# Down projection of two token groups as seven products in a stage of its own, its operands kept in device memory

## The chip, the core and the metric

The kernel runs on one NeuronCore of a Trainium2 chip. A core has a matrix engine (PE), which multiplies a stationary weight tile of 128x128 with a moving tile of 128 x n and adds into one of eight PSUM banks, three engines for elementwise work (DVE, ACT and POOL), and SP, which in this kernel only issues DMA transfers, in the order in which they stand on its queue. Each engine works through its own queue in order and waits on semaphores for the others. The metric is the device time of one execution in microseconds. Before the change the runs shown took 1119.27 and 1119.56 us, median 1119.41 us.

## The reference, cut to what matters

One layer of a decoder trunk for 1056 tokens (1024 of a prompt and 8x4 samples), D_MODEL = 1024, D_FF = 2816, all in fp32. The change lies in the last third of it:

```
def _rms(x, g):
    y = xf * lax.rsqrt(jnp.mean(xf * xf, axis=-1, keepdims=True) + EPS)
    return y * g

    ...                                     # mixing sub-layer gives x
    f = _rms(x, n_ffn_pre)
    f = (jax.nn.silu(f @ w_gate) * (f @ w_up)) @ w_down
    x = x + _rms(f, n_ffn_post)
    x = x + jax.nn.sigmoid(x @ w_ple_gate) * (p @ w_ple)
```

`w_gate` and `w_up` are 1024x2816, `w_down` is 2816x1024, `w_ple_gate` is 1024x1024, `w_ple` is 256x1024.

## The kernel before, in words

**Tiles.** Channels lie on the 128 partitions, tokens on the free axis. The 1056 tokens are three groups of 352: groups 0, 1 and 2. An fp32 product is made of three passes of a reduced format: every operand is split into a high part (a CAST on ACT, L164) and a low part (a subtraction on DVE, L165), and `gemm` (L291) issues for each 128x128 weight tile three matmuls of 128x352: high by high, high by low, low by high. In the profile a line "b<-hid,wh" is a matmul into a PSUM bank `b` with the moving tile `hid` (a hidden chunk) and the weight tile `wh`; "wl" is the low part of a weight, "fh" and "fl" the parts of the normalised input.

**Seven products.** Gate and up projection of groups 0 and 1 are made together: the two groups are the two columns, and two halves of 512 channels the two rows, of a 2x2 block product, which is made with seven block products in place of eight. Their operands are block sums made beforehand (`f7`: B11, B21, B22, T1 to T4), and the sums of weights come from POOL (`w_sums`, L1010). The same is done for the last product, x @ w_ple_gate, in the tail (`e7`, `ple_first`, `ple_rest`). Group 2 is always computed directly.

**The walk.** The 22 hidden chunks of 128 are taken in 11 slabs of two. `WALK` (L209) lists which slab is computed for which groups: slabs 0 to 4 for group 2; slabs 5 to 10 for all groups; slabs 0 to 4 for groups 0 and 1. For each item `gate_up` (L1026) makes the hidden chunk and writes it, split, to `hid`. Behind the first gate product of the next item `downs` (L1175) makes the down projection of the item before: for each of the eight output chunks m and each group in it, `down` (L1093) issues 2 chunks x 3 passes = 6 matmuls and adds the bank to the sum `o` (DVE, L1107; the first time a copy on ACT). So the down projection of groups 0 and 1 is 2 x 8 x 22 x 3 = 1056 matmuls, spread over the last eleven items, that of group 2 is 528.

**The tail.** When a group's sums are complete, `ple_steps` (L1136) makes its second normalisation: the squares are added up in `acc` (L813, L814), a ones matrix times `acc` on PE gives the mean (`rstd_steps`, L313), DVE scales (L1152), multiplies by the gain `gn` and adds the residual (L1156). The residual x was written to device memory earlier (`x1d<-x`) and is read back (`x<-x1d`, L1147). Then come the products with `w_ple_gate` and `w_ple`, the sigmoid, and the store of y.

**What sets the order.** PE runs its matmuls in the order written. `chain` puts the steps of a normalisation in line beside it: `turn(n)`, called behind each product, gives them n matmuls of progress, and a step that asks for 24 goes on when 24 matmuls have been issued. `need(k)` (L270) prepares weights ahead: it issues the load on SP (`w_load`, a raw tile `wr`, three slots), and the split of item k + LOOK on ACT and DVE. Raw tiles and `act_tile`s (tag "a", 28 slots of 128x1408) are reused, so a load or a split can wait for the last reader of a slot.

Of the kernel before, what the change touches and what calls it, by code (L numbers as in the profile page):

```python
# [10 lines left out]
F32 = mybir.dt.float32  # L11
F32R = mybir.dt.float32r
# [49 lines left out]
def trunk_kernel(  # L62
# [43 lines left out]
    def nm(s):  # L106
        cnt[0] += 1
        return f"{s}{cnt[0]}"
# [109 lines left out]
    def direct_item(src, shape):  # L218
        return item("direct", add_plan(src, shape))

    WGU, WD = [], []
    for s, gs in WALK:
        pairs_of = []
        for i in range(SLAB):
            c = SLAB * s + i
            jg = direct_item(w_gu[c, 0], [P, KC, P])
            if 0 not in gs:
                ju = direct_item(w_gu[c, 1], [P, KC, P])
            if i == 0 and WD:
# [7 lines left out]
        WD.append(None)  # L237
    WPE = [[], []]
# [5 lines left out]
    FIRST = 1  # L244
    for m in range(FIRST):
        plan_ple(0, m)
    WD[-1] = [direct_item(w_dn[WALK[-1][0], j], [P, SLAB, 512]) for j in range(2)]
    for m in range(FIRST, KC):
        plan_ple(0, m)


# [14 lines left out]
        W2[a] = wp0, item("half", jb), item("sums", ja, jb)  # L266

    made = {}

    def need(k, ahead=LOOK):  # L270

        for i in range(len(made), min(k + ahead + 1, len(ITEMS))):
            kind, js = ITEMS[i]
            if kind in ("direct", "home"):
                w_split(js[0], act_tile if kind == "home" else None)
                made[i] = pairs[js[0]]
            elif kind == "half":
                w_load(js[0])
                t = w_tile([P, KC, P], "w2")
                made[i] = t[:, 0:4, :], t[:, 4:8, :]  # L280
                split(*made[i], raws[js[0]][:, 4:8, :])
            else:
                for j in js:
                    w_load(j)
                made[i] = w_sums(*(raws[j] for j in js))
            for kind, js in ITEMS[i + 1 : i + 3]:
                for j in js:
                    w_load(j)
        return made[k]

    def gemm(ps, ops, start=True, stop=True):  # L291
# [698 lines left out]
    share[0] = 0.45  # L990


    hid = [None] * G

    new_hid = [None] * G

    def hid_put(g, slot, ht):
        split(new_hid[g][:, slot, :], new_hid[g][:, SLAB + slot, :], ht)

    def w_sums(a1, a2):  # L1000

# [21 lines left out]
    def quarter(w, h):  # L1023
        return tuple(t[:, 4 * h : 4 * h + 4, :] for t in w)

    def gate_up(items, slot, gs, pending):  # L1026

        ig, iu, is_ = items
        n = N

        def product(w, x):
            ps = bank()
            gemm(ps[:, :n], ops4(w, x))
            turn(12)
            return ps[:, :n]

        def direct(w):
            ps = bank()
            gemm(ps[:, :n], ops8(w, fs[2]))
            turn(24)  # L1040
            return ps[:, :n]

        def add(out, a, ps):
            ve.tensor_tensor(out, a, ps, op=ALU.add)
# [17 lines left out]
        for g in gs:  # L1062
            if slot == 0:
                new_hid[g] = half(g, F32R, "hid")
        if 2 in gs:
            hid_put(2, slot, sl)
# [8 lines left out]
        u3 = tmp(n, "u3")  # L1075
        add(u3, p1, product(s["S3"], f7["T3"]))
        c21 = tmp(n, "c21")
# [4 lines left out]
        hid_put(0, slot, c21)  # L1082
# [4 lines left out]
        se.activation(p1, p1, AF.Silu)  # L1087
        ve.tensor_tensor(u3, u3, p1, op=ALU.mult)
        hid_put(1, slot, u3)

    os_ = [None] * G

    def down(n, m, g):  # L1093
        wh, wl = need(WD[n][m // 4], 0 if n == len(WALK) - 1 else LOOK)
        cols = slice((m % 4) * P, (m % 4 + 1) * P)
        ps = bank()
        v = ps[:, : NS[g]]
        gemm(v, [(wh[:, k, cols], wl[:, k, cols], hid[g][:, k, :], hid[g][:, SLAB + k, :]) for k in range(SLAB)])
        turn(6)
        if os_[g] is None:  # L1100
            os_[g] = [half(g, s="o") for h in range(2)]
        o = os_[g][m // 4][:, m % 4, :]
        if (g, m) not in begun:
            begun.add((g, m))
            se.copy(o, v)
        else:
            ve.tensor_tensor(o, o, v, op=ALU.add)  # L1107
# [4 lines left out]
    pls = [None] * G  # L1112
    acc3 = [None] * G

    def last_down(n, m, g):
        down(n, m, g)
        if m == 0:
            acc3[g] = acc_tile(g)
        squares_into(acc3[g], os_[g][m // 4][:, m % 4, :], m == 0)


    e7 = {}
# [13 lines left out]
    def ple_steps(g):  # L1136
# [9 lines left out]
            x2[g][h] = half(g, s="x2")  # L1146
            nc.sync.dma_start(x2[g][h], x1d[g][h])  # L1147
        r = yield from rstd_steps(acc3[g], 28)
        behind = tc.keep_in_program_order if g == 2 else lambda ins: ins
        for h in range(2):  # L1150
            yh, xh = os_[g][h], x2[g][h]
            behind(ve.tensor_tensor(yh, yh, bc4(r), op=ALU.mult))  # L1152
            for c in range(4):
                k = 4 * h + c
                behind(
                    ve.scalar_tensor_tensor(  # L1156
                        xh[:, c, :], yh[:, c, :], gn[:, 3, k : k + 1], xh[:, c, :], op0=ALU.mult, op1=ALU.add
                    )
                )
                if g == 2 and c % 2:  # L1160
                    yield 6, 0
            yield 12 if g == 2 else 24, 0
            if g == 2:
                x2s[g].append(f_operand(xh, g))
            elif (g, h) != (1, 0):
                e7[f"B{h + 1}{g + 1}"] = f_operand(xh, g)
            yield 10, 0
# [2 lines left out]
                e_sum(name)  # L1170
                yield 20, 0

    END = len(WALK) - 1

    def downs(n):  # L1175
        s, gs = WALK[n]
        hid[:] = old_hid
        for half_m in (range(4), range(4, KC)):
            for g in (2, 0, 1):
                for m in half_m:  # L1180
                    if g in gs:
                        (last_down if g == 2 and s == NSLAB - 1 else down)(n, m, g)
        if s == NSLAB - 1:
            share[0] = 0.1
            chain(ple_steps(2), 19)

    for n, (s, gs) in enumerate(WALK):
        if n == AHEAD:
            finish(list(chains))
        old_hid = list(new_hid)  # L1190
        for i in range(SLAB):
            gate_up(WGU[n][i], i, gs, (lambda: downs(n - 1)) if i == 0 and n else None)
    finish(list(chains))
    share[0] = 0.7


    early = {}

# [85 lines left out]
            add(p1, p1, product(s["S4"], e7["B22"]))  # L1284
        ple_end(p1, wp, a, 1)

    hid[:] = new_hid
    for m in range(FIRST):
        ple_out(m, 2)
# [6 lines left out]
    for m in range(FIRST):  # L1296
        embed_early(WPE[0][m][0], m, 0)
    for m in range(FIRST, KC):
        ple_out(m, 2)
        embed_early(WPE[0][m][0], m, 0)  # L1300
    finish(chains[:1])
    for a in (7, 5, 3, 1):
        ple_first(a)
    for m in range(4):
# [90 lines left out]
```

## Time and profile before

| | |
|---|---|
| runs shown | 1119.27 and 1119.56 us, median 1119.41 |
| profiled execution | 1118.45 us, span 1116.7 us |
| granted clock of PE | 0.998 of full speed |
| PE busy | 1098.3 us, 98% of the span, 6999 instructions |
| DVE busy | 778.4 us, 70% |
| ACT busy | 458.8 us, 41% |
| POOL busy | 201.2 us, 18% |
| DMA | 101.79 MB, mean 91 GB/s |

A PE matmul line gives a mean of about 322 ns, but matmuls overlap in the pipeline, so the time that one costs is the distance between two starts, not its duration. The busy time of a window counts overlapping matmuls once. "PE b L126 <- DVE acc L814: 0.8, 1, 0.8" in the view of waits reads: matmuls of line 126 waited for the DVE instruction of line 814 that wrote `acc`, 0.8 us in all, once, at the longest 0.8 us.

### The profile page before, as it was taken

The numbers are of one execution on the slowest core, as the hardware profiler recorded it, in microseconds if no ns is written. First come the engines' busy times: TensorE is split into PE (matmuls) and PEld (weight loads), VectorE is DVE, ScalarE is ACT, GpSimd is POOL, SyncE is SP. The second block draws the span as 40 slices with busy tenths as digits, with TensorE's granted clock in tenths as the row PEclk, the third lists the DMA queues.
The fourth block names the chain that finished last, engine by engine and source line by source line (L and its number), as shares of the span: only waits on it lengthen the run. The fifth ranks groups of instructions, "written<-read, shape, count | busy, mean of one in ns | idle before, by whom it ended". The sixth has DMA issues, their size and how long they took to land.

```text
span 1116.7 us, 17519 instructions
## 1 busy us (share of the span) xinstructions
PE 1098.3 (98%) x6999; PEld 1080.0 (97%) x6999; DVE 778.4 (70%) x1296; ACT 458.8 (41%) x823; POOL 201.2 (18%) x169
## 2 busy tenths in 40 slices
PE   9999999999999999999999999999999999999987
PEld 8999988899999999999999999999999999999976
DVE  6766388877979864355565555657867877789887
ACT  8322268655645433331322213133424324366442
POOL 1045022100000221020111102012231132200242
PEclk9999999999999999999999999999999999999999
DMA  8121310542644212021120202114212212246242
GB/s 289 57 70 38 115 56 20 202 157 95 221 147 132 77 57 77 20 76 38 38 77 22 73 20 76 39 38 140 77 38 95 77 57 95 95 156 209 64 129 89
DMA packets 35986, 101.79 MB, mean 91 GB/s; under 512 B 4260, under 2 KB 14916, under 8 KB 35904
## 3 DMA queue, kind: packets, MB, share of 16 engines
q1 hardware_dynamic: 34576, 98.90, 26.3%
q10 hardware_dynamic: 1328, 1.77, 0.5%
q8 instruction: 55, 0.90, 0.3%
q14 instruction: 27, 0.22, 0.1%
HBM read 90.55 MB, written 10.11 MB: 90 GB/s over the span
## 4 chain that ended last, share of the span: by engine, by line
PE 82%; DVE 6%; POOL 3%; ACT 3%; issue 2%; DMA 2%; ACTq 0%; SPq 0%; POOLq 0%; DVEq 0%
PE b L126 81%; POOL wr L1010 3%; DVE wl L165 1%; DVE sl L165 1%; ACT sh L164 1%; DMA xr<-in_x_dram 1%; PE b L120 1%; DVE o L1133 1%; ACT h L394 1%; DVE sg L1223 1%; DVE yo L1225 1%; DMA wr<-in_w_pg_dram 0%; ACT wh L164 0%; DMA wr<-in_w_gu_dram 0%; ACT a L664 0%
## 5 line engine op out<-in xcount | busy, mean ns | idle before, releaser
L126 PE MATMUL b<-hid,wh 128*128 128x352 f32 x1056 | 253.1, 322 | 2.3 <-ACT hid L164 1.6
L164 ACT CAST wh<-wr 128x1024 fp32r<-128x1024 f32 (+1 forms) x135 | 138.8, 1030 | 252.7 <-PE b L126 203.4
L126 PE MATMUL b<-fh,wh 128*128 128x352 f32 x712 | 229.9, 323 | 0.0
L126 PE MATMUL b<-fh,wl 128*128 128x352 f32 x712 | 228.3, 321 | 0.0
L126 PE MATMUL b<-fl,wh 128*128 128x352 f32 x712 | 228.2, 320 | 0.0
L1010 POOL TENSOR_TENSOR wr<-wr 128x512 f32<-128x512 f32 x52 | 75.0, 1442 | 736.1 <-DVE wl L165 453.4
L165 DVE TENSOR_TENSOR wl<-wr,wh 128x1024 fp32r<-128x1024 f32 (+1 forms) x135 | 165.5, 1229 | 43.3 <-ACT wh L164 42.8
L126 PEld LDWEIGHTS b<-hid,wh 128*128 128x128 f32 x1056 | 182.7, 188 | 3.6 <-ACT hid L164 1.9
L126 PE MATMUL b<-hid,wl 128*128 128x352 f32 x528 | 169.3, 321 | 0.0
L126 PE MATMUL b<-fh,sh 128*128 128x352 f32 x416 | 134.7, 324 | 3.5 <-ACT sh L164 1.3
L126 PE MATMUL b<-fh,sl 128*128 128x352 f32 x416 | 133.7, 321 | 2.2 <-DVE sl L165 2.2
L1107 DVE TENSOR_TENSOR o<-o,b 128x352 f32<-128x352 f32 x240 | 115.3, 517 | 29.1 <-PE b L126 28.9
L126 PEld LDWEIGHTS b<-fl,wh 128*128 128x128 f32 x712 | 134.0, 188 | 0.0
L126 PEld LDWEIGHTS b<-fh,wh 128*128 128x128 f32 x712 | 133.5, 187 | 0.0
L126 PEld LDWEIGHTS b<-fh,wl 128*128 128x128 f32 x712 | 133.4, 187 | 0.0
L126 PE MATMUL b<-fl,sh 128*128 128x352 f32 x416 | 133.4, 321 | 0.0
L165 DVE TENSOR_TENSOR sl<-wr,sh 128x1024 fp32r<-128x1024 f32 x52 | 63.6, 1223 | 82.3 <-ACT sh L164 82.1
L164 ACT CAST sh<-wr 128x1024 fp32r<-128x1024 f32 x52 | 53.9, 1046 | 146.3 <-POOL wr L1010 103.2
L126 PE MATMUL b<-h,wh 128*128 128x352 f32 x480 | 105.5, 326 | 0.8 <-ACT h L394 0.8
L126 PEld LDWEIGHTS b<-hid,wl 128*128 128x128 f32 x528 | 98.9, 187 | 0.0
L126 PEld LDWEIGHTS b<-h,wh 128*128 128x128 f32 x480 | 82.6, 191 | 1.4 <-ACT h L394 1.1
L126 PEld LDWEIGHTS b<-fh,sh 128*128 128x128 f32 x416 | 78.0, 188 | 4.8 <-ACT sh L164 2.0
(186 smaller groups left out, 1680.2 us busy)
## 6 DMA issues: line engine op xcount, KB each, us to landing
wr<-in_w_gu_dram SPq DMA_DIRECT2D x64, 512.0 KB, 3.3
wr<-in_w_dn_dram SPq DMA_DIRECT2D x32, 512.0 KB, 3.9
wr<-in_w_pg_dram SPq DMA_DIRECT2D x18, 512.0 KB, 3.6
x<-in_x_dram SPq DMA_DIRECT2D x6, 704.0 KB, 9.1
x1d<-x SPq DMA_DIRECT2D x6, 704.0 KB, 3.9
x<-x1d SPq DMA_DIRECT2D x6, 704.0 KB, 6.2
out_y_dram<-yo SPq DMA_DIRECT2D x24, 176.0 KB, 1.9
wr<-in_w_out_b_dram SPq DMA_DIRECT2D x8, 512.0 KB, 3.3
```

Source lines behind the costliest of these rows:

```text
L120: ins = te.transpose(out, src, ident)
L126: ins = te.matmul(*args, **kw)
L164: fix(se.copy(hi, src))
L165: fix(ve.tensor_tensor(lo, src, hi.bitcast(F32), op=ALU.subtract))
L394: fix(se.activation(hi[:, c, :], t[:, c, :], AF.Identity, scale=gc))
L1010: ge.tensor_tensor(out, a, b, op=op)
L1107: ve.tensor_tensor(o, o, v, op=ALU.add)
L1133: ve.tensor_tensor(out, a, b, op=ALU.subtract)
L1223: ve.tensor_tensor(sg, sg, pp, op=ALU.mult)
L1225: ve.tensor_tensor(yo, sg, xm, op=ALU.add)
```

## The change

**Walk.** The five slabs taken first, for group 2 alone, are now 2, 4, 6, 8 and 10. Then the slabs go 0 to 10 in order: the even ones from 2 on with groups 0 and 1, the others with all three. Items with and without group 2 so alternate.

**Down projection of group 2** stays in the walk as it was (`down` without a group, L1185).

**Down projection of groups 0 and 1** leaves the walk. The two chunks of a slab are the two rows of the 2x2 block product. When a slab's hidden chunks are ready, `pair_put` makes the seven operands of the product (three of them as they are, four as differences on DVE), `stage` splits each into a high and a low part in a tile `st`, and when the tile holds two slabs it is written to device memory (`xd<-st`, L1070). Eleven slabs make six sets, the last with one slab: 7 x 5 writes of 704 KB and 7 of 352 KB.

**The stage behind the walk.** `STEPS` lists 19 steps, each a product (P1, P4, P2, S3, S2, S1, S4) over two sets, the last two over four. `down7` reads the operands back (`xo<-xd`, L1231, one step ahead), and for each of four output chunks issues 2 sets x 2 slabs x 3 passes = 12 matmuls (9 where one set has one slab) into a bank; DVE adds the bank to one of seven sums `u`. The total is 7 x 4 x 11 x 3 = 924 matmuls. In the last passes the sums are combined (L1270), `finished` adds the squares and multiplies by the gain (an ACT activation in place of the multiplication on DVE at L1156). The weights of the stage are quarters of `w_down` (`wq<-in_w_dn_dram`, L295, rows of 2 KB), their sums come from POOL (L316), and each is split on ACT and DVE (`qh`, `ql`).

**Chains.** The normalisation of group 2 now runs at the start of the stage, that of group 0 starts ahead of the last two steps, that of group 1 behind the last. All eight tail products of group 2 follow.

Instructions by kind: 128x352 matmuls 6516 before and 6384 now; DVE 1298 and 1305, ACT 769 and 865, POOL 174 and 198, SP 211 and 309.

```diff
     def tmp(n, s="t", dt=F32):
-        return spool.tile([P, n], dt, tag="tmp", bufs=6, name=nm(s), padded_shape=[P, NX])
+        return spool.tile([P, n], dt, tag="tmp", bufs=5, name=nm(s), padded_shape=[P, NX])
+    def kept(s):
+        return spool.tile([P, N], F32, tag="hk", bufs=4, name=nm(s))
...
-    WALK = [(s, (2,)) for s in range(AHEAD)]
-    WALK += [(s, (0, 1, 2)) for s in range(AHEAD, NSLAB)]
-    WALK += [(s, (0, 1)) for s in range(AHEAD)]
+    FIRST2 = tuple(range(NSLAB - 2 * AHEAD + 1, NSLAB, 2))
+    WALK = [(s, (2,)) for s in FIRST2]
+    WALK += [(s, (0, 1) if s in FIRST2 else (0, 1, 2)) for s in range(NSLAB)]
...
+    SETS = [list(range(i, min(i + 2, NSLAB))) for i in range(0, NSLAB, 2)]
+    OPERAND = {"P1": "B11", "P2": "B21", "P4": "T4", "S2": "T2", "S3": "T3", "S1": "T1", "S4": "B22"}
+    STEPS = [(k, (0, 1)) for k in FIVE + TWO]
+    STEPS += [(k, at) for at in ((2, 3), (4, 5)) for k in FIVE]
+    STEPS += [(k, (2, 3, 4, 5)) for k in TWO]
...
+    def stage(key, pair, src):
...
+        split(t[:, 0, i, :], t[:, 1, i, :], src)
+        if i == len(SETS[e]) - 1:
+            d = dpool.tile([P, 2, 2, N], F32, name=nm("xd"))
+            nc.sync.dma_start(d[:, :, : i + 1], t[:, :, : i + 1].bitcast(F32))
+            spilled[key, e] = d
+    def pair_put(pair, slot, h0, h1):
...
+        if slot == 0:
+            stage("B11", pair, h0)
+            sub(h0, h1, h0)
+            stage("T1", pair, h0)
+            evens[:] = h0, h1
+            return
+        t1, b12 = evens
+        stage("B21", pair, h0)
+        stage("B22", pair, h1)
+        sub(t1, h1, t1)
+        stage("T2", pair, t1)
+        sub(h0, h0, t1)
+        stage("T4", pair, h0)
+        sub(b12, h1, b12)
+        stage("T3", pair, b12)
...
         add(p1, p1, product(s["S4"], f7["B22"]))
         se.activation(p1, p1, AF.Silu)
         ve.tensor_tensor(u3, u3, p1, op=ALU.mult)
-        hid_put(1, slot, u3)
+        pair_put(pair, slot, c21, u3)
...
+    def finished(m, g):
...
+        squares_into(acc3[g], o, first)
+        se.activation(o, o, AF.Identity, scale=gn[:, 3, m : m + 1])
+    def x_get(n):
...
+                    nc.sync.dma_start(t[:, :, :w].bitcast(F32), spilled[key, e][:, :, :w])
+    def down7(n):
...
+        for i in range(n, n + 2):
+            x_get(i)
...
+            gemm(banks[j][:, :N], ops, e == at[0], e == at[-1])
+            turn(3 * len(ops))
...
+            add(u[k], u[k], v)
...
+            elif k == "S2":
+                add(u["P1"], u["P1"], u["S2"])
+                add(u["S3"], u["S3"], u["P1"])
+                add(u["P4"], u["P4"], u["S3"])
+                finished(4 + j, 0)
...
         r = yield from rstd_steps(acc3[g], 28)
...
-            behind(ve.tensor_tensor(yh, yh, bc4(r), op=ALU.mult))
-            for c in range(4):
...
+            ve.tensor_tensor(yh, yh, bc4(r), op=ALU.mult)
+            ve.tensor_tensor(xh, xh, yh, op=ALU.add)
+            yield 20, 0
...
+        if n == len(WALK) - 1:
+            x_get(0)
+    share[0] = 0.3
+    chain(ple_steps(2), 24)
+    for n in range(len(STEPS) - 2):
+        down7(n)
     finish(list(chains))
...
-    for m in range(KC):
-        last_down(END, m, 0)
-    chain(ple_steps(0), 24)
-    for m in range(KC):
-        last_down(END, m, 1)
-    chain(ple_steps(1), 54)
+    chain(ple_steps(0), 24)
+    down7(len(STEPS) - 2)
+    down7(len(STEPS) - 1)
+    share[0] = 0.7
+    chain(ple_steps(1), 24)
```

Two places where the order of the instructions matters for what follows. The first is SP's queue where the walk's products end. Before, the last two loads of `w_down` stand there, then loads for the tail (`wr` a raw weight tile, `pr` a part of p, `x<-x1d` the residual read back):

```order
L174 DMA wr_9474<-in_w_dn_dram 128x1024
L174 DMA wr_9547<-in_w_dn_dram 128x1024
L174 DMA wr_9584<-in_w_pg_dram 128x1024
L174 DMA wr_9603<-in_w_pg_dram 128x1024
L174 DMA wr_9676<-in_w_pg_dram 128x1024
L174 DMA wr_9683<-in_w_ple_dram 128x1024
```

Now the last writes of operands (`xd<-st`) stand there, and behind them the reads of the stage's first operands (`xo<-xd`):

```order
L1070 DMA xd_8500<-st_8497 256x1x352
L1070 DMA xd_8505<-st_8502 256x1x352
L1070 DMA xd_8511<-st_8508 256x1x352
L1070 DMA xd_8517<-st_8514 256x1x352
L1070 DMA xd_8523<-st_8520 256x1x352
L1231 DMA xo_8525<-xd_4825 128x1408
L1231 DMA xo_8527<-xd_5593 128x1408
L1231 DMA xo_8529<-xd_5026 128x1408
```

The four tiles st_8502, st_8508, st_8514 and st_8520 hold B22, T2, T4 and T3 of the last chunk; xo_8525 is the moving operand of the stage's first matmul, and the matmul before that one is the last product of the walk.

The second place is DVE's queue where group 0's sums are completed and its squares are added up. Before, each bank is added to `o` and the squares follow one product behind (`sq` are the squares, `acc` their sum):

```order
L1107 TENSOR_TENSOR o_4653<-o_4653,b_9765 128x352
L814 TENSOR_TENSOR acc_9730<-acc_9730,sq_9762 128x352
L1107 TENSOR_TENSOR o_4653<-o_4653,b_9776 128x352
L814 TENSOR_TENSOR acc_9730<-acc_9730,sq_9773 128x352
L1107 TENSOR_TENSOR o_4653<-o_4653,b_9787 128x352
L814 TENSOR_TENSOR acc_9730<-acc_9730,sq_9784 128x352
```

Now, in the last pass of S2, four additions follow each other for each output chunk, and splits of weights (`ql`, 128x1024 or 128x512) stand between them:

```order
L1270 TENSOR_TENSOR u_8844<-u_8844,b_9748 128x352
L1270 TENSOR_TENSOR u_8620<-u_8620,u_8769 128x352
L1270 TENSOR_TENSOR u_8533<-u_8533,u_8844 128x352
L168 TENSOR_TENSOR ql_9779<-wq_9220,qh_9778 128x1024
L874 TENSOR_TENSOR acc_9571<-acc_9571,sq_9744 128x352
L1270 TENSOR_TENSOR u_8769<-u_8769,u_8533 128x352
L168 TENSOR_TENSOR ql_9833<-wq_9234,qh_9832 128x512
L1270 TENSOR_TENSOR u_8620<-u_8620,u_8769 128x352
L168 TENSOR_TENSOR ql_9861<-wq_8927,qh_9860 128x1024
L874 TENSOR_TENSOR acc_9571<-acc_9571,sq_9762 128x352
```

In both versions 24 matmuls of 128x352 lie on PE between the last product that enters `acc` (bank b_9798 before, b_9748 now) and the matmul that reads `acc`.

More of the change, by code (lines that the diff above doesn't have):

```diff
@@ L242, in plan_ple @@
         WPE[n].append((wp, direct_item(w_pg[m], [P, KC, P])))
[L244 to L248, printed above, removed]
+    for m in range(KC):
         plan_ple(0, m)
@@ L268, in trunk_kernel, with q_load, q_loads, q_split @@
     made = {}
+    quarters = {}
+    def q_load(q, e):
+        if (q, e) not in quarters:
+            n = len(SETS[e])
+            shape = [P, n, 512]
+            if q == "11" and e > 1:
+                t = wpool.tile(shape, F32, tag="wr", bufs=W_RAW, name=nm("wq"))
+            else:
+                t = act_tile(shape, s="wq")
+            s0 = SETS[e][0]
+            row, col = int(q[1]) - 1, int(q[0]) - 1
+            nc.sync.dma_start(t, w_dn[s0 : s0 + n, col, :, row, :].rearrange("s p n -> p s n"))
+            quarters[q, e] = t
+        return quarters[q, e]
+    def q_loads(kind, js):
+        for q in {"P1": ("11",), "P4": ("22", "21"), "P2": ("12",)}.get(js[0], ()):
+            q_load(q, js[1])
+    def q_split(t):
+        hl = w_tile(t.shape, "qh"), w_tile(t.shape, "ql")
+        split(*hl, t)
+        return hl
+    def q_sum(k, e):
+        out, a, b, op = {
+            "S1": ("22", "21", "22", ALU.add),
+            "S3": ("21", "11", "21", ALU.subtract),
+            "S2": ("11", "22", "11", ALU.subtract),
+            "S4": ("12", "12", "11", ALU.subtract),
+        }[k]
+        ge.tensor_tensor(q_load(out, e), q_load(a, e), q_load(b, e), op=op)
     def need(k, ahead=LOOK):
@@ L281, in need @@
                 split(*made[i], raws[js[0]][:, 4:8, :])
+            elif kind == "quarter":
+                made[i] = q_split(q_load(QUARTER[js[0]], js[1]))
+                for n in {"P4": ("S1", "S3", "S2"), "P2": ("S4",)}.get(js[0], ()):
+                    for e in js[2]:
+                        q_sum(n, e)
+            elif kind == "dsum":
+                out = {"S1": "22", "S3": "21", "S2": "11", "S4": "12"}[js[0]]
+                made[i] = q_split(q_load(out, js[1]))
             else:
@@ L286, in need @@
             for kind, js in ITEMS[i + 1 : i + 3]:
-                for j in js:
-                    w_load(j)
+                if kind not in ("quarter", "dsum"):
+                    for j in js:
+                        w_load(j)
+            for kind, js in ITEMS[i + 1 : i + 7]:
+                if kind in ("quarter", "dsum"):
+                    q_loads(kind, js)
         return made[k]
@@ L1171, in ple_steps @@
                 yield 20, 0
-    END = len(WALK) - 1
     def downs(n):
-        s, gs = WALK[n]
         hid[:] = old_hid
[L1178 to L1185, printed above, removed]
+        for m in range(KC):
+            down(n, m)
+            if n == LAST2:
+                finished(m, 2)
     for n, (s, gs) in enumerate(WALK):
@@ L1191, in trunk_kernel @@
         for i in range(SLAB):
[L1192 removed]
+            first = i == 0 and n and 2 in WALK[n - 1][1]
+            gate_up(WGU[n][i], s, i, gs, (lambda: downs(n - 1)) if first else None)
+        if n == len(WALK) - 1:
[4 more added lines that the diff above has]
+        down7(n)
     finish(list(chains))
[L1194 removed]
     early = {}
```

137 lines of the change are left out of this document (94 added, 43 removed).

## The prediction

> **What bounds the kernel now.** I read the page's busy times first, then stages, then what PE waited for.
>
> ```profile
> PE 1098.3 (98%) x6999; PEld 1080.0 (97%) x6999; DVE 778.4 (70%) x1296; ACT 458.8 (41%) x823; POOL 201.2 (18%) x169
> ```
>
> PE is busy in 1098.3 of 1116.7 us. The windows say where the other 18.4 us are (window, its length, then busy time and count of PE, PEld, DVE, ACT, POOL, then clock, DMA share, GB/s):
>
> ```profile
> 0.00:30.00 30.00, 27.81 (x154) 26.90 (x154) 21.46 (x39) 25.15 (x44) 3.09 (x16) 1.00 0.75 269
> 390.00:750.00 360.00, 360.00 (x2267) 360.00 (x2267) 192.19 (x316) 99.78 (x152) 60.53 (x46) 1.00 0.16 50
> 806.00:905.00 99.00, 96.97 (x606) 96.04 (x606) 76.89 (x117) 36.05 (x50) 27.66 (x20) 1.00 0.22 70
> 905.00:1000.00 95.00, 94.72 (x590) 94.43 (x589) 74.08 (x128) 40.47 (x60) 16.75 (x12) 1.00 0.33 110
> 1000.00:1117.00 117.00, 104.12 (x643) 101.86 (x641) 99.21 (x142) 51.56 (x76) 23.43 (x16) 0.98 0.36 119
> ```
>
> From 390 to 750, most of the walk, PE is idle for nothing; the last 117 us have 12.9 us of idle, which is the end behind the last chains. So the bound is the count of matmuls, and the walk and the down projection have almost no slack to win from: what the change can win is matmuls, and what it can lose is idle time that PE does not have now. The waits in the whole trace are small:
>
> ```profile
> PE b L126 <- DVE sl L165: 2.2, 2, 1.5
> PE b L126 <- ACT hid L164: 1.6, 1, 1.6
> PE b L126 <- DVE acc L814: 0.8, 1, 0.8
> ```
>
> **Matmuls removed.** The direct down products of groups 0 and 1 are two thirds of these rows:
>
> ```profile
> L126 PE MATMUL b<-hid,wh 128*128 128x352 f32 x1056 | 253.1, 322 | 2.3 <-ACT hid L164 1.6 <-DVE o L1107 0.6
> L126 PE MATMUL b<-hid,wl 128*128 128x352 f32 x528 | 169.3, 321 | 0.0
> ```
>
> 1584 matmuls, 1056 of them for the two groups; seven products make 924 of those, 132 fewer. The mean of 322 ns is not their price, since they overlap. Of eight that follow each other, these are the first and the last:
>
> ```profile
> 977.82 0.33 PE L126 MATMUL b<-fh,wh 128*128 128x352 f32 x1
> ...
> 978.95 0.32 PE L126 MATMUL b<-fl,wh 128*128 128x352 f32 x1
> ```
>
> Seven steps in 1.13 us are 0.161 us each (the walk's window, 360 us by 2267, gives 0.159). So 132 x 0.161 = **-21.3 us**. That is 1.9% of the time: even with every wait hidden the kernel would hardly be faster by 2%, which is about what a measurement of it tells from no change.
>
> **The start of the stage.** In the order, the stage's first matmul follows the walk's last product directly. It needs xo_8525, and that read stands on SP's queue behind four writes which wait for the split operands of the last hidden chunk. These in turn hang on the walk's last product. So PE has nothing to do while a whole chain runs: eviction, silu, product, differences, splits, write issue, read. The durations are those of the like steps before (rows of DVE, then of ACT):
>
> ```profile
> 976.91 1.22 DVE L165 TENSOR_TENSOR wl<-wr,wh 128x1024 fp32r<-128x1024 f32 x1
> 978.05 0.52 DVE L1044 TENSOR_TENSOR p<-p,b 128x352 f32<-128x352 f32 x1
> 978.48 1.22 DVE L165 TENSOR_TENSOR wl<-wr,wh 128x1024 fp32r<-128x1024 f32 x1
> 979.61 0.52 DVE L1088 TENSOR_TENSOR u<-u,p 128x352 f32<-128x352 f32 x1
> 980.69 0.53 DVE L165 TENSOR_TENSOR hid<-u,hid 128x352 fp32r<-128x352 f32 x1 [0.55 <-ACT hid L164]
> ```
>
> ```profile
> 978.60 0.50 ACT L1087 ACTIVATE p<-p 128x352 f32<-128x352 f32 x1 [0.17 <-DVE p L1044]
> 980.17 0.49 ACT L164 CAST hid<-u 128x352 fp32r<-128x352 f32 x1 [1.07 <-DVE u L1088]
> ```
>
> By starts, a 128x352 step on DVE costs 0.43 us (978.05 to 978.48) and a 128x1024 split 1.14 us (976.91 to 978.05); a step that hands over to ACT and back adds about 0.55. On DVE's queue behind the walk's last product stand its addition, one 128x1024 split (silu runs beside it), the product, three differences and four low parts. That is 0.3 from PE to DVE, 9 x 0.43 + 1.14 = 5.0, and two handovers that the order doesn't hide, of about 0.4 to 0.55: 6.2 us. Then SP issues the last write and the first read, two instructions at some 0.4 us each:
>
> ```profile
> L1147 SPq DMA_DIRECT2D x<-x1d x6: 382/430/431, 775.6 to 1013.9; - x6
> ```
>
> so 0.8. The read is 704 KB, and landed transfers of that size are here:
>
> ```profile
> x<-in_x_dram SPq DMA_DIRECT2D x6, 704.0 KB, 9.1
> x1d<-x SPq DMA_DIRECT2D x6, 704.0 KB, 3.9
> x<-x1d SPq DMA_DIRECT2D x6, 704.0 KB, 6.2
> ```
>
> I take 6.2, the same kind of read, issued in pairs as here; 3.9 is a write in a quiet stage, 9.1 a read at the crowded start, and four writes of 352 KB are still under way before this one. Together **+13.2**, from 10.9 to 16.1. [...]
>
> **The clock after that wait.** PE's first microseconds, and a shorter pause near the end:
>
> ```profile
> 6.00:8.00 2.00, 2.00 (x7) 1.68 (x7) 2.00 (x5) 2.00 (x5) 0.00 (x0) 1.00 1.02 333
> 8.00:10.00 2.00, 2.00 (x9) 2.00 (x8) 1.66 (x3) 0.79 (x2) 0.00 (x0) 1.00 1.07 397
> 10.00:12.00 2.00, 2.00 (x15) 2.00 (x14) 1.14 (x3) 1.76 (x4) 0.00 (x0) 1.00 1.02 349
> ...
> 1084.00:1086.00 2.00, 0.59 (x2) 0.30 (x2) 0.73 (x2) 2.00 (x3) 0.00 (x0) 1.00 0.00 0
> ...
> 1088.00:1090.00 2.00, 2.00 (x15) 2.00 (x14) 2.00 (x5) 0.00 (x0) 0.38 (x1) 1.00 0.77 254
> ```
>
> After the long idle at the start two windows of 2 us hold 7 and 9 matmuls, later ones 15; after a pause of some 1.4 us at 1084 the next full window holds 15 at once. Against 30 in 4 us at full pace the 16 are 14 short, 2.2 us; I take **+1.4** for the one long wait, since part of those first ones may have been spaced by their operands (0 to 2.2).
>
> **Group 0's squares.** Before, 24 matmuls stand between the last product and the matmul that reads `acc`, and the longest wait for an `acc` is 0.8 us (row above). The 24 are still there, 3.9 us, but DVE now has four additions and one of squares per output chunk, with weight splits between. Counted from the start of the last S2 pass (36 matmuls, 5.8 us): four evictions of the step before to 0.7, two splits to 3.0, then on the queue up to the last `acc` 20 steps of 0.43 or a little more where one hangs on the one before, and splits of 1.14, 0.6 and 1.14: 3.0 + 20 x 0.45 + 2.9 = 14.9. PE is there at 5.8 + 3.9 = 9.7. **+5.2** (3 to 7, by whether DVE enters the pass late). Its cover before was that each product brought only two steps.
>
> **Group 1's squares.** Behind S4, PE has 12 matmuls of the last pass and 24 of the first tail product, 5.8 us. DVE from the first finished bank (0.6) has 12 steps and two splits: 0.6 + 12 x 0.47 + 2.3 = 8.5. **+2.7** (0 to 5).
>
> **The walk.** Its 2.3 us of waits before hidden operands (row above) go, as the next items are other ones. New are seven writes of 704 KB for each two slabs. Five of them stand on SP ahead of loads of the next chunks' weights; at 333 GB/s (row 6 to 8) they hold the transfer engines for 5 x 0.72 MB / 333 GB/s = 10.8 us, and items without group 2 bring no down products to cover a late weight. Loads run four items ahead, some 24 matmuls each, 4 x 3.9 = 15 us, so the margin is a few us. I take 0.8 late on each of the five, +4, less 2.3: **+1.7** (-2 to +10). DVE is at 192 of 360 us in the walk, so its new splits (0.43 each) have room, and the additions of `o` fall away:
>
> ```profile
> L1107 DVE TENSOR_TENSOR o<-o,b 128x352 f32<-128x352 f32 x240 | 115.3, 517 | 29.1 <-PE b L126 28.9
> ```
>
> 160 of 240 go, 69 us at 0.43; in the stage 48 additions to `u` and 28 sums of `u` come back, 33 us (the first 28 banks are copied by ACT).
>
> **Transfers in the stage.** The operands read are 35 x 704 KB + 7 x 352 KB = 27.8 MB; quarters of `w_down` not yet loaded about 5.8 MB, residuals and tail weights some 4.4: 38 MB in 924 x 0.161 = 149 us, 255 GB/s. The window 0 to 30 moved 269 GB/s at a share of 0.75, so it fits with a quarter spare; a step reads one step ahead, 36 matmuls or 5.8 us against 6.2 us to land. **+1** (0 to 6).
>
> **The tail** has the same chains and products; DVE has six additions of 128x1408 for 24 multiplications at L1156. They lie beside idle PE in part: 0 (-3 to +3).
>
> **Sum:** -21.3 + 13.2 + 1.4 + 5.2 + 2.7 + 1.7 + 1.0 = +3.9. The profiled execution of 1118.45 becomes 1122.4; the median stands 0.96 above it, so **1123**. With the parts' bounds taken as independent, the case reaches from about 1116 to 1135.
>
> **Rivals.** *The waits are short, the gain stands.* DVE keeps up at both sums, the walk loses its 2.3 and gains nothing, the first read lands in 3.9: -21.3 + 10.9 - 2.3 = -12.7, about 1107. For it speaks that PE waits so little for DVE now; against it the order, where the chain at the stage's start has no other work beside it. *The transfers pace the stage (slower).* Every matmul of the stage has a moving operand fresh from device memory. It decides below 255 GB/s; the last window moved 119 on the mean, 254 in its best quoted 2 us. At 200 GB/s the 38 MB take 190 us, 41 more than the products, which swallow the two sums' waits: -21.3 + 13.2 + 1.4 + 1.7 + 41 = +36, about 1155. Against it are the 333 to 397 GB/s of the first rows. *The clock falls after each wait.* If every pause of some microseconds is followed by the slow start seen at 6 us, the waits at the start and at both sums cost 2.2 each, 6.6 in place of 1.4: about 1128.5. The 1.4 us pause does not show it, and no longer one is in the trace behind the start. [...] That the change doesn't save its matmuls is no rival: the order has 132 fewer.
>
> **Chances.** Forecast 0.55, short waits 0.18, transfers 0.09, clock 0.10, anything else 0.08. The range 1103 to 1140 leaves out the transfers, the low end of the short waits and half of the rest, some 0.17. Faster by over 2% (below 1097) needs nearly all waits gone: 0.03. Slower (above 1141.8) is the transfers and a little of the rest: 0.10. Within 2%: 0.87.
>
> **What would show it.** A wait of PE on a transfer `xo` of 11 to 16 us where the walk ends; PE on DVE `acc` of about 5 and 3 us; `hid,wh` down to 352 and 924 matmuls on `xo`; a DMA share in the stage of 0.6 to 0.8 with no further waits on `xo`. Many waits on `xo` of a microsecond or more would mean that the transfers pace the stage; a first wait below 8 us would break the largest term, and waits on weights in the walk the next.

## The result, and the profile after

The changed kernel takes 1152.99 us (1151.57 to 1154.42, two runs) where the kernel before takes 1119.41: a ratio of 1.030, 95% interval 1.0245 to 1.0355. It is 33.6 us slower. The forecast was 1123 with a range of 1103 to 1140, so the time lies outside, on the slow side. Its size is near that of the rival in which transfers pace the stage (1155), but that is not what the trace shows.

The page of the changed kernel, busy times and the slices of PE and of its clock:

```profile
span 1152.6 us, 17678 instructions
...
PE 1092.3 (95%) x6867; PEld 1070.8 (93%) x6867; DVE 858.1 (74%) x1303; ACT 508.9 (44%) x919; POOL 266.2 (23%) x193
...
PE   8999999999999999999999999999819999789997
...
PEclk9999999999999999999999999999869999899998
```

PE has 132 instructions fewer, and is idle 60.3 us of its span in place of 18.4. What it waited for (us in all, times, longest):

```profile
PE b L126 <- DMA xo<-xd: 25.5, 1, 25.5
PE b L126 <- DVE acc L874: 11.8, 3, 7.4
PE b L126 <- ACT sh L167: 5.8, 5, 3.3
PE b L126 <- DVE sl L168: 3.2, 6, 0.7
```

`xo` appears once. Of 616 + 308 matmuls with an operand from device memory only the first waited for it, so the stage is not paced by its transfers; the costliest groups say the same (busy, mean ns, then idle before it):

```profile
L126 PE MATMUL b<-xo,qh 128*128 128x352 f32 x616 | 150.1, 327 | 25.5 <-DMA xo<-xd 25.5
L126 PE MATMUL b<-xo,ql 128*128 128x352 f32 x308 | 100.3, 326 | 0.2 <-DVE ql L168 0.2
```

**The first wait.** The chain behind the walk's last product is the one that the prediction walked through, but its steps are not as long as it took them to be. DVE in the changed kernel, start and duration:

```profile
841.50 3.15 DVE L168 TENSOR_TENSOR ql<-wq,qh 128x1024 fp32r<-128x1024 f32 x1
844.58 2.66 DVE L1182 TENSOR_TENSOR u<-u,p 128x352 f32<-128x352 f32 x1
847.27 2.55 DVE L1078 TENSOR_TENSOR c<-u,c 128x352 f32<-128x352 f32 x1
849.74 2.67 DVE L1078 TENSOR_TENSOR u<-u,u 128x352 f32<-128x352 f32 x1
852.33 2.65 DVE L168 TENSOR_TENSOR st<-u,st 128x352 fp32r<-128x352 f32 x1
854.91 2.65 DVE L168 TENSOR_TENSOR st<-c,st 128x352 fp32r<-128x352 f32 x1
857.49 0.51 DVE L1078 TENSOR_TENSOR c<-c,c 128x352 f32<-128x352 f32 x1
```

Five 128x352 steps in a row take 2.55 to 2.67 us each, and at 857 the same kind takes 0.51 again. POOL at that time makes the first sums of weights of the stage:

```profile
841.23 15.95 POOL L316 TENSOR_TENSOR wq<-wq,wq 128x1024 f32<-128x1024 f32 x6 [12.99 <-DVE ql L168]
```

Six sums in 15.95 us, 2.66 each, and over at 857.2: each of the five steps took about the length of one POOL sum. In this trace the slow steps differ from the others by where their inputs lie. From 923.7 to 947.6 POOL makes eight more sums, and DVE's steps with one input in a PSUM bank `b` go on at their pace beside them, while a split of weights (1.2 us alone), with both inputs in SBUF, takes 3:

```profile
932.86 0.51 DVE L1270 TENSOR_TENSOR u<-u,b 128x352 f32<-128x352 f32 x1
933.29 2.99 DVE L168 TENSOR_TENSOR ql<-wq,qh 128x1024 fp32r<-128x1024 f32 x1
936.20 1.37 DVE L1270 TENSOR_TENSOR u<-u,b 128x352 f32<-128x352 f32 x3
```

Over the whole trace, of DVE's 128x352 steps (TENSOR_TENSOR) that begin while one of POOL is under way and at least 0.1 us before its end, all 64 with both inputs in SBUF took longer (0.70 to 2.67 us), and none of the 82 with an input in a bank did (at most 0.53). SP shows who stood behind DVE:

```profile
834.61 25.67 SPq L1070 DMA_DIRECT2D xd<-st  x6
860.37 2.29 SPq L1231 DMA_DIRECT2D xo<-xd  x4
```

The last write is issued at 860.3, the first read at 860.4, and PE starts on it at 866.0.

**The clock.** Behind some waits of this trace PE is slow for a while. PE in the walk, right behind two short waits:

```profile
666.15 0.43 PE L126 MATMUL b<-fh,sh 128*128 128x352 f32 x1 [1.34 <-ACT sh L167]
...
667.41 0.43 PE L126 MATMUL b<-fh,sl 128*128 128x352 f32 x1 [0.67 <-DVE sl L168]
...
668.56 0.50 PE L126 MATMUL b<-fh,sl 128*128 128x352 f32 x1
668.85 0.50 PE L126 MATMUL b<-fh,sh 128*128 128x352 f32 x1
```

and the windows around them (the granted clock is the third figure from the end):

```profile
664.00:668.00 4.00, 2.00 (x11) 1.41 (x10) 1.87 (x3) 2.95 (x5) 1.02 (x1) 1.00 0.00 0
668.00:672.00 4.00, 4.00 (x18) 4.00 (x17) 3.50 (x6) 2.71 (x4) 0.00 (x0) 0.57 0.81 238
672.00:676.00 4.00, 4.00 (x27) 4.00 (x26) 3.83 (x5) 0.00 (x0) 2.63 (x3) 1.00 0.08 29
```

From 668.6 to 671.8 the distance between starts is 0.29 us in place of 0.161, and the granted clock of that window is 0.57. The trace has seven such stretches, which cost 1.6 to 2.7 us each: one at the start, as in the kernel before, and six that are new, at 666, 829, 866, 1002, 1036 and 1135.

**The account** of the profiled executions, spans 1116.7 and 1152.6: PE's idle time grew by 41.9. Of this 25.5 is the first wait, 11.1 the two waits on `acc`, 8.5 the walk (its gaps sum to 10.7 where those before sum to 2.2), and -3.2 the tail (2.4 in place of 5.6). PE's busy time fell by only 6.0 where 21.3 of matmuls went, which leaves 15.3. Some 11.6 of these are the slower clock in the six new stretches; the other 3.7 I cannot put at a place.

### The profile page after: what moved, and what is told of

Its sections match the earlier page's. It is cut to its first block, busy times and chain, and to the rows that moved or that the text cites. A ratio compares the mean times of both kernels' runs of the same rounds, so it can differ in the third digit from the quotient of the medians.

```text
span 1152.6 us, 17678 instructions
## 1 busy us (share of the span) xinstructions
PE 1092.3 (95%) x6867; PEld 1070.8 (93%) x6867; DVE 858.1 (74%) x1303; ACT 508.9 (44%) x919; POOL 266.2 (23%) x193
## 4 chain that ended last, share of the span: by engine, by line
PE 72%; DVE 11%; DMA 5%; ACT 4%; POOL 4%; issue 3%; POOLq 0%; SPq 0%; ACTq 0%; DVEq 0%
PE b L126 71%; POOL wr L1106 4%; DMA wr<-in_w_gu_dram 2%; DVE st L168 2%; DVE u L1270 2%; DVE wl L168 1%; ACT wh L167 1%; DVE ql L168 1%; DVE sl L168 1%; DMA xr<-in_x_dram 1%; ACT sh L167 1%; PE b L120 1%; DVE acc L874 1%; ACT h L454 1%; DMA xo<-xd 0%
## 5 line engine op out<-in xcount | busy, mean ns | idle before, releaser
L167 ACT CAST wh<-wr 128x1024 fp32r<-128x1024 f32 (+1 forms) x125 | 128.3, 1028 | 192.0 <-PE b L126 122.4
L168 DVE TENSOR_TENSOR wl<-wr,wh 128x1024 fp32r<-128x1024 f32 (+1 forms) x125 | 153.1, 1227 | 35.3 <-ACT wh L167 34.7
L126 PE MATMUL b<-xo,qh 128*128 128x352 f32 x616 | 150.1, 327 | 25.5 <-DMA xo<-xd 25.5
L126 PE MATMUL b<-fh,sh 128*128 128x352 f32 x416 | 137.3, 330 | 8.2 <-ACT sh L167 5.8
L126 PE MATMUL b<-fh,sl 128*128 128x352 f32 x416 | 136.8, 329 | 3.2 <-DVE sl L168 3.2
L126 PEld LDWEIGHTS b<-xo,qh 128*128 128x128 f32 x616 | 108.9, 192 | 25.8 <-issue 25.8
L126 PE MATMUL b<-xo,ql 128*128 128x352 f32 x308 | 100.3, 326 | 0.2 <-DVE ql L168 0.2
L126 PE MATMUL b<-hid,wh 128*128 128x352 f32 x352 | 84.3, 322 | 1.6 <-DVE c L1140 1.6
L126 PEld LDWEIGHTS b<-fh,sl 128*128 128x128 f32 x416 | 80.2, 193 | 5.1 <-DVE sl L168 5.1
L168 DVE TENSOR_TENSOR ql<-wq,qh 128x1024 fp32r<-128x1024 f32 (+1 forms) x42 | 61.8, 1491 | 30.6 <-ACT qh L167 18.2
```

The source lines that it names most:

```text
L126: ins = te.matmul(*args, **kw)
L167: fix(se.copy(hi, src))
L168: fix(ve.tensor_tensor(lo, src, hi.bitcast(F32), op=ALU.subtract))
```

## The experiments

**The first wait: POOL, or something else.** The first six sums of weights wait for a one-column copy on POOL that reads the stage's first operand; nothing else is changed.

```diff
+                        if js[0] == "P4" and e < 2:
+                            late.append((n, e))
+                        else:
+                            q_sum(n, e)
...
+            tc.keep_in_program_order(ge.tensor_copy(gate, xops[OPERAND[k], at[0]][:, 0, 0, 0:1].bitcast(F32)))
+            for q in late:
+                tc.keep_in_program_order(q_sum(*q))
```

> Only the first six sums of weights on POOL wait, by a one-column copy on POOL that reads the stage's first operand, until that operand has landed. Theory 'lock': DVE steps with two operands in SBUF stood still while POOL ran its six sums of 2.66 us back to back; without them beside it the chain at the walk's end runs at 0.43 to 0.55 us a step and the first wait on xo falls from 25.5 to about 13, the time from 1153 to about 1140. Rival 'traffic': the steps were slow because of the transfers under way, POOL has nothing to do with it; the wait stays at 25 and the steps at 2.6. The delayed sums may give a new wait on weight splits of a few us at the fourth product.

1144.92 us, 1.0231 of the kernel before [1.0198, 1.0265]. The wait:

```profile
PE b L126 <- DMA xo<-xd: 13.2, 1, 13.2
```

and the same steps of DVE:

```profile
844.52 0.52 DVE L1186 TENSOR_TENSOR u<-u,p 128x352 f32<-128x352 f32 x1
845.07 0.53 DVE L1082 TENSOR_TENSOR c<-u,c 128x352 f32<-128x352 f32 x1
845.51 0.52 DVE L1082 TENSOR_TENSOR u<-u,u 128x352 f32<-128x352 f32 x1
845.95 0.52 DVE L168 TENSOR_TENSOR st<-u,st 128x352 fp32r<-128x352 f32 x1
```

With POOL quiet the steps are 0.52 us, and the wait is 13.2, the prediction's own figure. The other 12.3 are POOL's. The time fell by 8.1 where 13 were expected: this run's trace has eight slow stretches behind the start in place of six, 3.3 us more, and the rest is within the spread of two runs.

**Reads ahead of the last writes.**

```diff
         t1, b12 = evens
+        if pair == NSLAB - 1:
+            x_get(0)
+            x_get(1)
         stage("B21", pair, h0)
```

> Only the reads of the first two steps' operands are issued ahead of the last chunk's writes. Theory 'queue': the first wait on xo is the place of the read behind the writes on SP's queue; it falls from 25.5 to below 1, and a new one appears at the third step, whose reads still stand behind the last write: that one is issued at about 860 in the changed kernel, lands at 866, and PE comes there about 856, so about 10 us. Time about 1153 - 15 = 1138. Rival 'transfers': the reads are slow whatever their place, the first wait stays above 5.

1140.01 us, 1.0187 [1.0142, 1.0232]. The time is as expected, the place of the remaining wait is not:

```profile
PE b L126 <- DMA xo<-xd: 3.7, 3, 1.8
PE b L126 <- DVE dg L397: 7.2, 2, 7.0
```

The first read now waits 1.3, just above what was expected, and the third step 2.4. In front of that stands a wait of 7.0 that I had not seen: the scaling of group 2 (`dg`), whose steps lie on DVE behind the slowed chain. The 10 us are there, but their releaser is DVE. So the first wait was the read's place on SP, and behind it stands the same chain of DVE.

**Both together.** Here POOL's sums wait for the walk's last split (`st` of T3) and not for the read, which now lands earlier.

> The reads of the first two steps stand ahead of the last chunk's writes, and the first six sums of weights on POOL wait for the last split of the walk. Theory 'lock and queue are the whole of the first wait': the first wait on xo and those behind it fall below 2 us together, group 2's scaling (dg) no longer waits 7.0, the time falls from 1153 to about 1126, that is 25 us for the wait and 2 for the slow matmuls behind it. Rival: the sums, now later, make the weight splits of the fourth and fifth product late, and half of the gain comes back as waits on ql or qh.

1141.72 us, 1.0203 [1.0182, 1.0223]: no better than the reads alone, where 1126 was expected. The rival holds in kind, but not for the whole of the loss. The wait on the first operand is gone, and this stands in its place:

```profile
PE b L126 <- DVE ql L168: 6.7, 3, 3.6
```

A window of that run:

```profile
850.00:860.00 10.00, 9.75 (x62) 9.46 (x60) 10.00 (x5) 3.85 (x6) 10.00 (x4) 1.00 1.01 381
```

DVE (third pair of figures) makes five steps in 10 us beside POOL's four: the sums now stand beside the splits of weights. These waits give back 6.5 us. PE's idle time fell by 17.7 all the same (60.3 to 42.6), but its busy time grew by 4.6 (1092.3 to 1096.9), and what of this is not slow stretches is open.

**More cover ahead of the two sums.**

```diff
-    chain(ple_steps(0), 24)
+    chain(ple_steps(0), 72)
...
-    chain(ple_steps(1), 24)
+    chain(ple_steps(1), 54)
```

> Only the cover between the last product that enters acc and the matmul that reads acc changes: 72 matmuls for group 0 and 54 for group 1 in place of 24. Theory 'late sums': the waits of 7.4 and 3.7 us go below 1 each, and with them the slow matmuls behind each (about 1.75 each): time from 1153 to about 1139. Rival 'DVE bound': DVE is behind in that stretch as a whole, the waits move to the steps behind (the operands of the tail) and the time stays within 4 us.

1139.89 us, 1.0186 [1.0149, 1.0223]: 13.1 less. The wait on `acc` is 0.7 in all, which is the one in the first part that the kernel before has too, and the two slow stretches behind the old waits are gone with them. The one at 666 is missing too, behind pauses of 1.36 and 0.67 that are still there; the edit, far behind that place, has no part in this, and it is 1.7 us of the gain. DVE is busy nearly throughout there (a window), but PE no longer waits for it:

```profile
980.00:1000.00 20.00, 19.76 (x125) 19.34 (x124) 19.97 (x36) 12.60 (x22) 0.00 (x0) 1.00 0.89 324
```

**The walk: a blocked queue, or bandwidth.** The writes are held and issued behind the next chunk's loads of weights.

```diff
+            if i:
+                held.append((d, t, i))
+            else:
+                nc.sync.dma_start(d[:, :, : i + 1], t[:, :, : i + 1].bitcast(F32))
...
         s = need(is_)
+        spill()
         add(p1, p1, product(s["S2"], f7["T2"]))
```

`spill()` issues the writes held, in the order written.

> In the walk the writes of a chunk's operands are issued on SP behind the next chunk's loads of weights, not ahead of them. Theory 'blocked queue': SP stands for up to 12 us at a write that waits for the last split, and the loads behind it are late; PE's waits on the weight sums (sh, sl) in the walk, 9.0 us together, fall below 2, with the slow matmuls behind them (about 4 us): time from 1153 to about 1141. Rival 'bandwidth': the loads are late because the writes fill the transfer engines; the waits stay as they are.

1143.49 us, 1.0218 [1.0185, 1.0251]: 9.5 less. SP in the changed kernel, in one of the places:

```profile
639.24 10.15 SPq L1070 DMA_DIRECT2D xd<-st  x5
650.58 17.13 SPq L177 DMA_DIRECT2D wr<-in_w_gu_dram  x3
```

SP stood 10 us at the five writes. With the writes later the waits on sums of weights are

```profile
PE b L126 <- DVE sl L168: 2.0, 3, 0.7
PE b L126 <- ACT sh L167: 0.4, 1, 0.4
```

9.0 became 2.4, just above the 2 expected, at the same number of bytes: it was the queue. The first wait of the stage grew to 28.9 here: DVE came out of the walk later, its last split ends 22.6 us behind the walk's last product in place of 19.0, and the read follows it as before.

**The walk's order.** The changed kernel with the order of slabs of before; the sets of operands follow that order.

```diff
-    WALK = [(s, (2,)) for s in FIRST2]
-    WALK += [(s, (0, 1) if s in FIRST2 else (0, 1, 2)) for s in range(NSLAB)]
+    WALK = [(s, (2,)) for s in range(AHEAD)]
+    WALK += [(s, (0, 1, 2)) for s in range(AHEAD, NSLAB)]
+    WALK += [(s, (0, 1)) for s in range(AHEAD)]
```

> The changed kernel with the walk's order of before (slabs 0 to 4 for group 2, 5 to 10 for all, 0 to 4 for groups 0 and 1); the sets of operands follow that order. Theory 'items without group 2 have too little cover': five such items in a row have no group 2 products between the loads, so the waits on weight sums (sh, sl) move into those items and grow from 9 to about 15 us, time about 1158. Rival 'order is of no account': the same waits behind each pair of slabs, time within 3 us of 1153.

1158.25 us, 1.035 [1.033, 1.0371], 5.3 more than the changed kernel. The waits on `sh` and `sl` do move into the five items without group 2 (from 705 us on), but grow only from 9.0 to 11.2; four slow stretches follow there in place of two. The alternation is worth some 5 us, and is not what made the kernel slow.

**All four edits.**

> All four edits together: reads ahead, first sums on POOL behind the walk's last split, 72 and 54 matmuls of cover ahead of the two matmuls that read acc, and the writes in the walk behind the next loads. Theory 'the loss is four separate waits and the slow clock behind them': they add up, 1153 - 27 - 14 - 10 = 1102, 1.5% faster than the kernel before, near the 21.3 us that the missing matmuls are worth. Rival 'transfers': with PE no longer standing, the stage asks for its operands faster and waits on xo appear; the time stays above 1112.

1113.78 us, 0.9958 [0.9943, 0.9974]: 0.4% faster than the kernel before, but 12 short of the sum. One long wait is left, 10.9 us on the first `xo`. Its SP queue says why:

```profile
805.72 14.11 SPq L296 DMA_DIRECT2D wq<-in_w_dn_dram  x4
819.88 5.08 SPq L1084 DMA_DIRECT2D xd<-st  x5
825.06 2.47 SPq L1077 DMA_DIRECT2D xd<-st  x2
827.62 4.89 SPq L1249 DMA_DIRECT2D xo<-xd  x4
```

Four loads of `w_down` block SP for 14 us, one of them a prefetch for the second pair of sets that waits for a raw slot; the held writes and the reads come behind. So the transfer engines are nearly empty at first, and then everything comes at once (share and GB/s are the last two figures):

```profile
810.00:820.00 10.00, 9.13 (x55) 8.55 (x54) 9.24 (x14) 5.46 (x10) 5.84 (x4) 1.00 0.04 11
825.00:835.00 10.00, 1.73 (x11) 1.44 (x9) 9.73 (x17) 3.69 (x7) 0.00 (x0) 0.74 1.03 417
```

The first read is issued at 827.6, and PE starts on it at 837.6, 10 us later, where the changed kernel needed 5.6 (860.4 to 866.0). It is a wait on `xo` behind full transfer engines, as the rival said, but they are full because the blocked queue had bunched the transfers.

**Order of the transfers kept as written.** The five writes of the fifth set stand ahead of those loads, the reads of the first two steps ahead of the seven writes of the last set, and all of the stage's transfers are issued in the order written.

> As the kernel with all four edits, but the transfers of the stage keep the order written: the five writes of the fifth set stand ahead of the loads that blocked SP for 14 us, and the reads of the first two steps ahead of all seven writes of the last set. Theory 'place on SP's queue': the wait of 10.9 on the first xo falls below 2, a wait of about 2 may appear at the third step; with the slow matmuls behind it the time falls from 1113.8 to about 1102. The six POOL sums run from the last split on beside weight splits on DVE; theory 'lock' expects waits on ql of about 5 us there, as with the two edits alone (6.7), so 1107. Rival 'the transfers are too many at that place': the wait on xo only moves to the second and third step and the time stays at 1112 to 1115.

1121.2 us, 1.0019 [1.0005, 1.0033]: the first wait fell to 1.5, and two new ones cost more.

```profile
PE b L126 <- DMA xo<-xd: 10.6, 3, 8.6
PE b L126 <- DVE dg L401: 7.0, 3, 6.5
```

The 8.6 stands at 923 us: two prefetches of `w_down`, now pinned ahead of the reads, hold SP for 33.9 us. The 6.5 is group 2's scaling again.

**The sums on DVE.** The same kernel with the six sums on DVE in place of POOL.

> As the run before, but these six sums of weights are made on DVE (six steps of 1.14 us behind the walk's last split) and not on POOL. Theory 'lock': the splits beside them run at 1.14 to 1.23 us, none at 2.6 or more, and the waits on ql at the stage's start fall below 1.5: 3 to 5 us less than the run before, about 1102. Rival 'DVE has too much to do there': DVE is no faster through the stretch, the waits on ql stay, same time within 2 us.

1126.9 us, 1.0072 [1.0047, 1.0096]: 5.7 more, which neither the theory nor the rival had. There was nothing to win on `ql`, for which PE waits only 0.2 us in the pinned kernel. The six sums take 6.89 us on DVE and not the 14 to 16 on POOL, but they stand ahead of group 2's steps, and the wait on `dg` grows to 10.5:

```profile
837.17 6.89 DVE L317 TENSOR_TENSOR wq<-wq,wq 128x1024 f32<-128x1024 f32 x6
...
847.26 2.31 DVE L391 TENSOR_TENSOR hl<-sd,hl 128x3 fp32r<-128x3 f32 x1
```

The second row is one of them: a subtraction of 128x3 that took 2.31 us (0.16 in the changed kernel) beside POOL's next two sums.

**Order free again, and group 2 later.** As the pinned kernel, but only the transfers up to the second step keep their order, and `chain(ple_steps(2), 24)` becomes 216.

> As the pinned kernel with the sums on POOL, but only the transfers up to the first two steps keep the order written, and group 2's normalisation starts 216 matmuls into the stage in place of 24. Theory: the wait of 6.5 on dg came from DVE's steps beside POOL's sums, right after the walk, and goes with the later place; the wait of 8.6 on xo came from two loads of w_down that blocked SP for 34 us, and goes with the order left free. Both below 1.5, with the slow matmuls behind them: 1121 - 19 = about 1102, 1.6% faster than the kernel before. Rival: SP is blocked by some other load in their place, or the splits beside the sums are late; the time stays above 1110.

1102.61 us, 0.9854 [0.9838, 0.9871], where 1102 was expected. The waits on `xo` are 2.1 in all, that on `dg` 0.5, and PE is idle 19.4 us of a span of 1102.3. Of the 21.3 us of matmuls 16.5 are in the time. The two rows that follow are windows of this run:

```profile
840.00:860.00 20.00, 18.43 (x104) 17.92 (x103) 14.12 (x6) 7.67 (x13) 20.00 (x7) 0.91 1.02 395
860.00:880.00 20.00, 20.00 (x130) 20.00 (x129) 12.31 (x15) 11.20 (x18) 1.68 (x1) 1.00 1.03 405
```

The transfer engines are full here for 40 us, at 395 and 405 GB/s and a share of 1.02 and 1.03, and PE stands still for 1.6 of them: at the stage's start the transfers have nothing to spare, but over all of it they keep up (a share of 0.37 to 0.86 in the windows of 20 us from 880 to 1020).

## Why the prediction was wrong, point by point

**Matmuls, -21.3: right.** 132 went, and the kernel in which the waits are gone is faster by 16.5 of them.

Two terms failed, the start by 12.3 us and the clock by some 10. The first alone would have given 1135, inside the range.

**The start, +13.2: the first term that failed.** The chain, its place and its length without POOL beside it were right: 13.2 without POOL's sums. That the figure agrees to a tenth is luck: to the last split, to the read's issue and to its landing it is 6.6, 0.9 and 5.7, where 6.2, 0.8 and 6.2 were taken. The step that failed is "by starts, a 128x352 step on DVE costs 0.43 us". The steps were priced from rows beside which POOL was idle, and the change puts six POOL sums of 2.66 us at just that place; they were never laid beside the chain. The rows before could have warned: among the 22 steps u<-u,p of L1088 the shortest takes 518 ns, the middle one 521 and the longest 926, which the mean of 540 hides. That one began while POOL made a sum of weights:

```profile
809.06 2.83 POOL L1010 TENSOR_TENSOR wr<-wr,wr 128x512 f32<-128x512 f32 x2
809.80 0.93 DVE L1088 TENSOR_TENSOR u<-u,p 128x352 f32<-128x352 f32 x1
```

Term measured: 25.5. The trace has 2.55 to 2.67 us for a 0.52 us step with both inputs in SBUF beside sums of 2.66, and 0.51 for a step with one input in PSUM (932.86); what makes the two kinds differ it does not show. Had the split and the five steps that began beside the six sums been put at the measured 2.66 us each in place of 1.14 and 0.43, the term would have been an estimated 13.2 + 6 x 2.66 - (1.14 + 5 x 0.43) = 26.

**The clock, +1.4: the second term that failed, too small by some 10.** Measured are 11.6 in six stretches. The price of one was somewhat low (1.6 to 2.7 measured). The step that failed was that only the one long wait pays. Six places paid: the first wait, both waits on `acc`, one of 3.3 and a pair of 1.34 and 0.67 in the walk, and one of 2.35 in the tail. Of the "clock" rival the slow starts came, but not from the three waits it named alone. The stretch from 668.6 lasts 3.2 us. In the traces of all kernels here, PE waits 29 times for 3.3 us or more, and a slow stretch follows each time. Less was enough in some places and not in others: of nine waits of 2.3 to 2.4 us six have one behind them; 1.34 and 0.67 us, with two matmuls between, were enough at 667, while 1.36 and 0.67 at the same place of the run with more cover and 1.3 and 1.5 us at 1084 in the kernel before were not.

**Group 0's and group 1's squares, +5.2 and +2.7: right in kind, short in size.** They measured 7.4 and 3.7, the first just above its range of 3 to 7; the larger cover removed both. Why DVE was later than counted was not followed.

**The walk, +1.7: too small.** It measured 8.5 within the range of -2 to +10, for another reason than the one priced: not 10.8 us of transfers ahead of the loads, but SP standing at a write that waits for DVE's last split.

**Transfers in the stage, +1: right, the term measured 0.** The rival that gave 1155 came near the time by chance: no product but the first waited for an `xo` in the changed kernel. **The tail, 0:** -3.2, just outside its -3 to +3, and not explained. The chance of slower by over 2%, 0.10, was far too low; the costs were priced one by one and taken as independent, although a wait at one place brought a slow clock behind it in six places of the changed kernel's trace, and POOL and SP are shared by all of them.

## What to carry to other kernels

Price a step at the place to which the change moves it, with what the other engines do there: a chain on DVE whose steps have both inputs in SBUF and that stands beside a run of POOL sums took here about a POOL sum per step (2.55 to 2.67 us beside 2.66), and the maximum of a row told this (926 ns) where its mean did not (540). A transfer on SP's in-order queue that waited for a late result delayed the loads behind it (10 us at five writes in the walk; with the writes later PE's waits there fell from 9.0 to 2.4), so writes of results belong behind the loads that others need, and prefetches behind both. Where a change trades 2% of the matmuls for new hand-overs, count the waits on PE twice: each one of 3.3 us or more was paid in these traces as idle time and again in the clock behind it (1.6 to 2.7 us a stretch in the changed kernel), and shorter ones sometimes.

## What the runs showed of the hardware that was not expected

A 128x352 DVE step with both inputs in SBUF took 2.55 to 2.67 us beside a run of POOL sums of 2.66 us, and 0.52 without; even a 128x3 subtraction took 2.31 in the run with the sums on DVE (0.16 in the changed kernel). Of the changed kernel's 128x352 steps that began beside one of POOL's, at least 0.1 us before its end, all 64 with both inputs in SBUF took 0.70 to 2.67 us, and all 82 with one input in PSUM stayed at 0.51 to 0.53. All 29 waits of PE of 3.3 us or more, over twelve traces, were followed by a slow clock, and six of nine of 2.3 to 2.4; so were some pairs of shorter ones, like 1.34 and 0.67 us (granted clock 0.57 in a window of 4 us right behind them). Transfers ran at 395 to 405 GB/s (a share of 1.02 and 1.03) for 40 us with PE and DVE at work.
